# Attention softmax with eight score tiles instead of seven, one reciprocal tile instead of two, and no pad

## The chip, the cores and the metric

The kernel runs on one core of a Trainium2 chip. The metric is the time of one execution on the device in microseconds (us); less is better. The core has a matrix engine (TensorE, PE in the profile; PEld is its loading of weights, which overlaps with its matmuls), three engines for element-wise work (VectorE or DVE, ScalarE or ACT, GpSimd or POOL) and SyncE (SP), which here only issues transfers. POOL issues transfers too. Each engine takes its instructions in order. SBUF is the memory on the core that the engines work in, PSUM the one that matmuls write to.

## The reference

Two layers on a stream of 1024 latent positions and 256 context positions of width 1024, in float32. Layer 0 is attention, layer 1 a state-space mixer that the change does not touch. Around each stand a modulated RMS normalization and a gated residual add. The attention has 16 heads of 64 in four groups that share keys and values:

```python
s = jnp.einsum('bqkgd,bskd->bkgqs', qb, kb).astype(jnp.float32) * scale
p = sink_softmax(s, sink_kg, mask).astype(vb.dtype)
return jnp.einsum('bkgqs,bskd->bqkgd', p, vb)
...
y_lat = ((o * jax.nn.silu(g)) @ w_out).astype(h_lat.dtype)
```

A block of 128 latent queries looks at up to three blocks of 128 latent keys around it and at the two context blocks; context queries look at the context alone. `sink_softmax` adds one more logit per head to the sum of the exponentials.

## The kernel before

A product of two float32 matrices is made from three matmuls over a high and a low part of each operand: ACT rounds a weight tile to its high part (`split_w`, line 221) and DVE or POOL subtracts (line 223).

The attention works in 40 units, one for each block of 128 queries and each of the four key groups. The first 8 are context units with two key blocks each, the other 32 are latent units with four or five. A unit has two halves.

`att_front` (line 740) loads the unit's queries through POOL's queue (lines 748 and 753) and its gates through SP's (749). Then, for each of the four heads r of the group, PE computes the scores S in PSUM (lines 767 and 768; two S buffers), DVE scales, masks and reduces them to `sm` in SBUF (line 772) and ACT makes the exponential in place with its sum (774). A short chain follows: the sink's share (777, 778), the sum (779), its reciprocal (781) and a copy of the reciprocals spread out by POOL (`rs`, 782).

`att_back` (line 785) goes over the key blocks. PE transposes the four `sm` tiles' part of the block into `pt` (793; two buffers), ACT rounds it (`ph`, 797), DVE takes the low part (`pl`, 798), and PE multiplies both with the values into `pv` (799, 800). After the last block PE transposes `rs` (806), and DVE, ACT and POOL put the output of the unit together, with the reciprocals and the gates (807 to 816).

The main loop of `attention` (line 930) writes `att_front` of unit x+1 and then `att_back` of unit x. After each key block `tick` (903) advances a filler: the q and gate projections of the second half of the latent positions, and later the output projection of the blocks that are done (`proj_g`, lines 238 to 240; weights by `load_halves`, 245). The output projection of the last 512 positions comes behind the units; its weights are loaded into buffers of the tag `sm` (line 228, `spare`).

The order on each engine is not that of the program text. A planner at build time takes, for each engine, the instruction that was written first among those that it expects to be ready; the filler has a higher priority and may not be ahead of a given matmul (`issue_after`). It also places the waits. A tile's tag has a number of buffers (`BUFS`, line 41), which its tiles take in turn; a tile can be written once the tile that had its buffer before has been read for the last time. `sm` has 7 buffers of 2560 bytes per partition, `rs` has 2 of 1024 bytes. The pool `att` begins with a tile `pad` of 1536 bytes (line 826) that nothing writes or reads.

Of the kernel before, what the change touches and what calls it, by code (L numbers as in the profile page):

```python
# [9 lines left out]
F32 = mybir.dt.float32  # L10
# [7 lines left out]
P = 128  # L18
# [11 lines left out]
HD = 64  # L30
# [10 lines left out]
BUFS = dict(  # L41
    wr=2, wh=2, wl=2, arow=1, rr512=2, sqt=3, ut=3, ar=3, ah=2, al=2,
    pj=1, S=2, pt=2, pv=1,
    rope_b=2, qf=3, qh=3, ql=2, kHH=2, kLL=2, qs=2, sgt=2, sm=7, mx=2, nm=2, es=2, sums=2, ph=2, pl=2, co=1, ot=2,
    oraw=3, h1=2, h1k=8, wada=6, gq=1, sqa=1,
    cacc=2, cctx=1, bT=2, cT=2, xn4=4, xn2=1, bn4=4, bn2=1, sz=2, xw=2, hf=2, hx=2, M=2, bw=2, y2=1, xs=1, uT=2, pj2=2, psX=3, sk=2, dg=2,
)
# [66 lines left out]
class Kernel:  # L114
# [13 lines left out]
    def t(self, pool, shape, dt, tag, bufs=None):  # L128
        self.n += 1
        kw = {"bufs": bufs or BUFS.get(tag, 1)}  # L130
        return pool.tile(shape, dt, tag=tag, name=f"{tag}_{self.n}", **kw)
# [608 lines left out]
    def att_front(self, p, x, i, j, b):  # L740
        nc, t = self.nc, self.t
        ps = self.psA
        o = b * P - TT[i][0]
        sg = t(self.psm, [P, 2, P], F32, "sgt")
        nm = t(p, [P, R], F32, "nm")
        sums = t(p, [P, R], F32, "sums")
        qs = t(p, [P, R, P], F32R, "qs")
        nc.gpsimd.dma_start(qs, self.q_d[j][i][:, :, :, o : o + P].rearrange("e s d n -> (s d) e n"))
        nc.sync.dma_start(sg, self.sg_d[j][i][:, :, o : o + P].rearrange("e p n -> p e n"))

        z = j % 2
        qz = self.qz[z]
        nc.gpsimd.dma_start(qz[z * HD : (z + 1) * HD], self.q_d[j][i][:, z, :, o : o + P].rearrange("e d n -> d e n"))
        if b < 8:
            k0, k1 = max(b - 1, 0), min(b + 2, 8)
        else:
            k0, k1 = 8, 8
        kb = list(range(k0, k1)) + [8, 9]
        c0_ = 512 - (k1 - k0) * P
        m0 = {0: 128, 7: 640}.get(b, 0 if b < 8 else 384)  # L760
        W = len(kb) * P
        sms = []
        for r in range(R):
            S = t(self.psS, [P, 1024], F32, "S")
            for x, (qq, kk) in enumerate(((qs[:, r, :], self.kHH[j]), (qz[:, r, :], self.kL[j // 2]))):
                if k1 > k0:
                    nc.tensor.matmul(S[:, c0_:512], qq, kk[:, k0 * P : k1 * P], start=x == 0, stop=x == 1)  # L767
                scored = nc.tensor.matmul(S[:, 512:768], qq, kk[:, LAT : LAT + CTX], start=x == 0, stop=x == 1)  # L768
            self.scored.append(scored.ins)
            Sv = S[:, c0_:768]  # L770
            sm = t(self.psm, [P, 640], F32, "sm")
            nc.vector.tensor_tensor_reduce(out=sm[:, :W], in0=Sv, in1=self.mask[:, m0 : m0 + W], scale=-SCALE, scalar=self.nsink[:, 4 * j + r : 4 * j + r + 1],  # L772
                                           op0=ALU.add, op1=ALU.min, accum_out=nm[:, r : r + 1])
            nc.scalar.activation(sm[:, :W], sm[:, :W], AF.Exp, bias=nm[:, r : r + 1], scale=-1.0, accum_out=sums[:, r : r + 1])  # L774
            sms.append(sm)
        es = t(p, [P, R], F32, "es")
        nc.gpsimd.tensor_tensor(es, nm, self.sink[:, 4 * j : 4 * j + 4], op=ALU.add)
        nc.scalar.activation(es, es, AF.Exp)
        nc.gpsimd.tensor_tensor(sums, sums, es, op=ALU.add)
        rs = t(self.pb, [P, 2, 2, HD], F32, "rs", 2)  # L780
        nc.vector.reciprocal(sums, sums)
        nc.gpsimd.tensor_copy(rs, sums.rearrange("p (x e) -> p e x", e=2).unsqueeze(3).broadcast_to([P, 2, 2, HD]))
        return j, b, i, o, kb, sms, sg, rs
# [34 lines left out]
    def attention(self, c0, ckv):  # L818
        nc, t, a = self.nc, self.t, self.a
# [3 lines left out]
        self.psm = self.pool("sm", ctx=c0)  # L823
        self.pb = self.pool("back", ctx=c0)
        p = self.pool("att", ctx=c0)
        t(p, [P, 384], F32, "pad")
        cq = ExitStack()
        pq = self.pq = self.pool("qp1", ctx=cq)
        BUFS.update(qf=2, rope_b=1, qh=1, ql=1)
# [986 lines left out]
```

## Time and profile before

| | us |
|---|---|
| median of 3 runs | 1782.68 |
| lowest, highest | 1781.32, 1782.68 |
| the profiled execution, its time | 1780.27 |
| its span, first to last instruction | 1778.4 |

The mean granted clock of TensorE in the profiled execution is 0.996 of full speed. The attention's units begin at about 248 us and the transposes of the last end at about 676 us.

The profile names an instruction by its line (L793), engine, operation and tiles (written tile <- read tiles; 128x512 is partitions by elements). A row "A <- B: total, times, longest" says that instructions A waited for B, and how long. Rows in order of time have the start and the length in us, and in brackets the idle time of the engine ahead of the instruction, with what ended it. The ends of matmuls are modelled; a PE that is busy is not one at its peak.

### The profile page before, as it was taken

What the parts mean: (1) busy time and instruction counts of PE and PEld (TensorE: products, weight loads), DVE (VectorE), ACT (ScalarE), POOL (GpSimd) and SP (SyncE); (2) the same over time, 40 slices, a digit from 0 to 9 for tenths busy, and PEclk for the clock granted to TensorE, in tenths of its full rate; (3) what the DMA queues carried; (4) which work ended last, traced back from release to release, by engine and by line L of the source; (5) the groups of instructions that cost most, each with busy time, mean ns of one, the idle gap of its engine ahead of it and who ended that gap; (6) DMA issues with size and microseconds to landing.
All of it is one profiled execution on the core that took longest, in us unless ns stands there. A gap on an engine that the chain in (4) does not pass through costs nothing.

```text
span 1778.4 us, 29177 instructions
## 1 busy us (share of the span) xinstructions
PE 1739.9 (98%) x10413; PEld 1505.5 (85%) x10413; DVE 1204.2 (68%) x2119; ACT 871.8 (49%) x1902; POOL 796.8 (45%) x1066
## 2 busy tenths in 40 slices
PE   9999999999999999999999999999999999999997
PEld 6897788888888787778898898989889898988887
DVE  5744446788877875684876867677685767876634
ACT  4522247777777774352444444344443434544522
POOL 3231047555565545103454553636455363554321
PEclk9999999999999999999999999999999999999998
DMA  9478855444455446222323233332333333655533
GB/s 361 169 216 256 293 145 143 101 103 106 113 151 132 117 109 217 74 64 63 81 73 91 81 81 84 83 82 72 92 81 76 89 81 80 180 165 168 182 102 117
DMA packets 211388, 225.53 MB, mean 127 GB/s; under 512 B 15788, under 2 KB 149036, under 8 KB 211244
## 3 DMA queue, kind: packets, MB, share of 16 engines
q1 hardware_dynamic: 177180, 205.02, 39.0%
q0 software_dynamic: 34064, 18.65, 5.7%
q8 instruction: 82, 1.34, 0.3%
q14 instruction: 62, 0.51, 0.1%
HBM read 188.78 MB, written 35.13 MB: 126 GB/s over the span
## 4 chain that ended last, share of the span: by engine, by line
PE 84%; DVE 8%; DMA 2%; ACT 2%; issue 2%; POOL 1%; SPq 0%; DVEq 0%; ACTq 0%; POOLq 0%
PE pj L1213 18%; PE pj L1247 10%; PE pj L1648 7%; PE pj L238 6%; PE pj L239 6%; PE pj L240 6%; PE psD L1198 4%; PE psX L1400 3%; PE pt L793 3%; PE psD L1316 2%; PE pv L800 2%; PE psX L1369 2%; PE psX L1368 2%; PE pv L799 2%; PE S L767 1%
## 5 line engine op out<-in xcount | busy, mean ns | idle before, releaser
L238 PE MATMUL pj<-uH,wh 128*128 128x512 f32 (+1 forms) x680 | 244.1, 359 | 3.9 <-DVE h L859 2.0
L240 PE MATMUL pj<-uH,wl 128*128 128x512 f32 (+1 forms) x680 | 230.1, 339 | 1.4 <-POOL wl L223 1.4
L239 PE MATMUL pj<-uL,wh 128*128 128x512 f32 (+1 forms) x680 | 230.5, 339 | 0.4 <-POOL uL L816 0.4
L1213 PE MATMUL pj<-uH,wh 128*128 128x512 f32 x512 | 173.8, 411 | 1.2 <-ACT bn L1168 1.2
L1213 PE MATMUL pj<-uH,wl 128*128 128x512 f32 x512 | 170.4, 403 | 0.0
L1213 PE MATMUL pj<-uL,wh 128*128 128x512 f32 x512 | 168.2, 403 | 0.0
L1291 POOL TENSOR_TENSOR xw<-xn,dtdec 128x256 f32<-128x256 f32 x144 | 95.5, 664 | 160.4 <-PE psD L1316 75.8
L238 PEld LDWEIGHTS pj<-uH,wh 128*128 128x128 f32 x680 | 129.3, 190 | 28.0 <-ACT wh L221 5.7
L1247 PE MATMUL pj<-wh,uH 128*128 128x256 f32 x512 | 150.7, 294 | 0.0
L1247 PE MATMUL pj<-wl,uH 128*128 128x256 f32 x512 | 150.5, 294 | 0.0
L1247 PE MATMUL pj<-wh,uL 128*128 128x256 f32 x512 | 150.2, 293 | 0.0
L798 DVE TENSOR_TENSOR pl<-pt,ph 128x512 fp32r<-128x512 f32 x168 | 114.0, 688 | 47.2 <-ACT ph L797 46.2
L240 PEld LDWEIGHTS pj<-uH,wl 128*128 128x128 f32 x680 | 128.8, 190 | 17.3 <-POOL wl L223 2.2
L239 PEld LDWEIGHTS pj<-uL,wh 128*128 128x128 f32 x680 | 129.7, 191 | 10.5 <-issue 1.1
L223 POOL TENSOR_TENSOR wl<-wr,wh 128x512 fp32r<-128x512 f32 x74 | 97.2, 1316 | 84.7 <-ACT wh L221 83.8
L772 DVE CUSTOM_DVE_ANT_0 sm<-S,mask,nsink 128x640 f32<-128x640 f32 (+2 forms) x160 | 119.2, 772 | 20.6 <-PE S L768 13.5
L1432 ACT ACTIVATE uT<-psX,nw 128x128 f32<-128x128 f32 x128 | 46.5, 363 | 171.7 <-PE psX L1431 167.7
L774 ACT ACTIVATE sm<-sm,nm 128x640 f32<-128x640 f32 (+2 forms) x160 | 118.7, 742 | 17.5 <-DVE nm L772 16.9
L797 ACT CAST ph<-pt 128x512 fp32r<-128x512 f32 x168 | 97.4, 585 | 56.7 <-PE pt L793 52.4
L221 ACT CAST wh<-wr 128x512 fp32r<-128x512 f32 (+1 forms) x116 | 74.5, 648 | 81.8 <-PE pj L239 58.4
L1213 PEld LDWEIGHTS pj<-uH,wl 128*128 128x128 f32 x512 | 96.0, 188 | 19.9
L1213 PEld LDWEIGHTS pj<-uL,wh 128*128 128x128 f32 x512 | 95.5, 188 | 19.2
(352 smaller groups left out, 4945.3 us busy)
## 6 DMA issues: line engine op xcount, KB each, us to landing
wr<-w_x SPq DMA_DIRECT2D x32, 512.0 KB, 4.2
M<-acs SPq DMA_DIRECT2D x64, 256.0 KB, 5.3
bw<-acs SPq DMA_DIRECT2D x64, 256.0 KB, 5.6
wr<-w_sk SPq DMA_DIRECT2D x24, 512.0 KB, 4.1
wr<-wg SPq DMA_DIRECT2D x40, 256.0 KB, 5.2
qs<-q POOLq DMA_DIRECT2D x40, 256.0 KB, 3.9
wada<-w_ada SPq DMA_DIRECT2D x16, 512.0 KB, 8.6
wr<-wq SPq DMA_DIRECT2D x32, 256.0 KB, 3.1
```

The costliest lines, as they stand in the source:

```text
L223: (eng or nc.vector).tensor_tensor(l, raw, h, op=ALU.subtract)
L238: self.nc.tensor.matmul(ps, lh, rh, start=first and i == 0, stop=False)
L239: self.nc.tensor.matmul(ps, lh, rl, start=False, stop=False)
L240: self.last_mm = self.nc.tensor.matmul(ps, ll, rh, start=False, stop=last and i == n - 1)
L772: nc.vector.tensor_tensor_reduce(out=sm[:, :W], in0=Sv, in1=self.mask[:, m0 : m0 + W], scale=-SCALE, scalar=self.nsink[:, 4 * j + r : 4 * ...
L774: nc.scalar.activation(sm[:, :W], sm[:, :W], AF.Exp, bias=nm[:, r : r + 1], scale=-1.0, accum_out=sums[:, r : r + 1])
L797: nc.scalar.copy(ph, ptf)
L798: nc.vector.tensor_sub(pl, ptf, ph)
L1213: self.pe = nc.tensor.matmul(raw[:, 512 * i : 512 * i + 512], l[:, k, :], r[i][:, k, :], start=k + y == 0, stop=k == KT - 1 and y == 2)
L1247: self.pe = nc.tensor.matmul(pj[:, c], l, r[:, k, :], start=c % 2 + q + k + y == 0, stop=c % 2 == 1 and q == 1 and k == 3 and y == 2)
L1291: nc.gpsimd.tensor_tensor(xw, X(st, c).rearrange("p (r h) -> p r h", r=R), self.dtdec[:, c, hd(d, g)].unsqueeze(2).broadcast_to([P, R, HP] ...
L1648: self.pe = nc.tensor.matmul(banks[x], l[:, z, sl], r, start=k == 2 * qs[0] and y == 0, stop=k == 2 * qs[-1] + 1 and y == 2)
```

## The change

Three edits, all in the attention. The number of `sm` buffers goes from 7 to 8. The tile `rs` takes the default number of buffers of a tag without an entry, which is 1, in place of 2. The `pad` tile goes. Seven tiles of 2560 bytes, two of 1024 and the pad of 1536 are as many bytes as eight of 2560 and one of 1024. The planner plans the whole program again.

```diff
-    ... ql=2, kHH=2, kLL=2, qs=2, sgt=2, sm=7, mx=2, nm=2, es=2, sums=2, ph=2, pl=2, co=1, ot=2,
+    ... ql=2, kHH=2, kLL=2, qs=2, sgt=2, sm=8, mx=2, nm=2, es=2, sums=2, ph=2, pl=2, co=1, ot=2,
...
-        rs = t(self.pb, [P, 2, 2, HD], F32, "rs", 2)
+        rs = t(self.pb, [P, 2, 2, HD], F32, "rs")
         nc.vector.reciprocal(sums, sums)
         nc.gpsimd.tensor_copy(rs, sums.rearrange("p (x e) -> p e x", e=2).unsqueeze(3).broadcast_to([P, 2, 2, HD]))
...
         p = self.pool("att", ctx=c0)
-        t(p, [P, 384], F32, "pad")
         cq = ExitStack()
```

More of the change, by code (lines that the diff above doesn't have):

```diff
@@ L43 @@
     pj=1, S=2, pt=2, pv=1,
-    rope_b=2, qf=3, qh=3, ql=2, kHH=2, kLL=2, qs=2, sgt=2, sm=7, mx=2, nm=2, es=2, sums=2, ph=2, pl=2, co=1, ot=2,
+    rope_b=2, qf=3, qh=3, ql=2, kHH=2, kLL=2, qs=2, sgt=2, sm=8, mx=2, nm=2, es=2, sums=2, ph=2, pl=2, co=1, ot=2,
     oraw=3, h1=2, h1k=8, wada=6, gq=1, sqa=1,
```

## The prediction

> **What bounds the kernel now.** I read the page first, then the engines' busy time by stretch, then who waited for whom inside the attention, then one unit of it in order of time.
>
> ```profile
> PE 1739.9 (98%) x10413; PEld 1505.5 (85%) x10413; DVE 1204.2 (68%) x2119; ACT 871.8 (49%) x1902; POOL 796.8 (45%) x1066
> ...
> PE 84%; DVE 8%; DMA 2%; ACT 2%; issue 2%; POOL 1%; SPq 0%; DVEq 0%; ACTq 0%; POOLq 0%
> ```
>
> TensorE (PE) is busy in 98% of the span and holds 84% of the chain that ended last. The change touches the attention alone, so only its stretches matter. In the next view the columns are the length, then PE, weight loads, DVE, ACT and POOL busy, each with its instructions.
>
> ```profile
> 248.00:295.00 47.00, 45.59 (x249) 37.76 (x248) 30.80 (x100) 34.57 (x103) 32.29 (x52) 1.00 0.60 142
> 295.00:670.00 375.00, 364.05 (x2173) 310.89 (x2171) 292.34 (x622) 273.49 (x606) 214.07 (x306) 1.00 0.48 117
> 670.00:720.00 50.00, 46.93 (x206) 36.55 (x207) 31.06 (x40) 22.16 (x39) 25.75 (x21) 1.00 0.60 195
> ```
>
> The first row is the eight context units, the second the 32 latent units, the third the output projection behind them. PE idles 1.41, 10.95 and 3.07 us, together 15.4 us, 0.9% of the run. That is all that a better order can give back, unless it takes out work, and this change takes out none. DVE at 78% of the long stretch comes second.
>
> What PE waits for in the long stretch (total, times, longest; all six rows):
>
> ```profile
> PE pv L800 <- DVE pl L798: 5.4, 12, 1.9
> PE pj L238 <- DVE h L859: 2.0, 2, 1.6
> PE S L767 <- DVE nm L772: 0.7, 2, 0.5
> PE pv L799 <- DVE ot L812: 0.7, 1, 0.7
> PE pt L380 <- DVE dg L378: 0.4, 1, 0.4
> PE pv L799 <- ACT ph L797: 0.3, 1, 0.3
> ```
>
> No row has the transposes (L793) waiting for a softmax tile, which is what an eighth tile would serve.
>
> **The change part by part.** A unit u has four softmax tiles r0 to r3. Taking seven buffers in turn, the nth tile gets the buffer of tile n-7: r3 of unit u+1 that of r0 of unit u, and r0 of u+2 that of r1 of u. These come free when the last key block of u is transposed. The trace has it, in the order of time (start, length, and in brackets the idle time before):
>
> ```profile
> 427.26 0.60 PE L793 MATMUL pt<-ident,sm 128*128 128x128 f32 x4
> ...
> 427.57 0.88 DVE L772 CUSTOM_DVE_ANT_0 sm<-S,mask,nsink 128x640 f32<-128x640 f32 x1 [0.62 <-PE pt L793]
> ...
> 428.38 0.88 DVE L772 CUSTOM_DVE_ANT_0 sm<-S,mask,nsink 128x640 f32<-128x640 f32 x1
> ...
> 428.50 0.83 ACT L774 ACTIVATE sm<-sm,nm 128x640 f32<-128x640 f32 x1
> ...
> 428.85 0.38 PE L806 MATMUL pt<-ident,rs 128*128 128x128 f32 x2
> ...
> 429.19 0.68 DVE L798 TENSOR_TENSOR pl<-pt,ph 128x512 fp32r<-128x512 f32 x1
> ...
> 430.35 0.40 POOL L782 COPY rs<-sums 128x256 f32<-128x256 f32 x1 [0.56 <-DVE sums L781]
> ...
> 430.56 0.88 DVE L772 CUSTOM_DVE_ANT_0 sm<-S,mask,nsink 128x640 f32<-128x640 f32 x1 [0.27 <-PE S L768]
> ...
> 431.40 0.89 DVE L772 CUSTOM_DVE_ANT_0 sm<-S,mask,nsink 128x640 f32<-128x640 f32 x1
> ...
> 431.43 0.60 PE L793 MATMUL pt<-ident,sm 128*128 128x128 f32 x4
> ...
> 433.52 0.83 ACT L774 ACTIVATE sm<-sm,nm 128x640 f32<-128x640 f32 x1
> ...
> 434.67 0.50 PE L800 MATMUL pv<-pl,v 128*128 128x512 f32 x1
> ```
>
> The first transpose of the last block lets the reduction at 427.57 go: r3 of u+1; 428.38 is r0 of u+2; 430.56 and 431.40 are r1 and r2 of u+2, as soon as a score buffer S (there are two) is free again.
>
> *The eighth tile.* With eight, r0 of u+2 takes the buffer of r0 of u, and r3 of u+1 takes one that came free a whole unit earlier. So at 427.57 and 428.38 stand r0 and r1, at 430.56 and 431.40 r2 and r3. It is the same row of four reductions, set off by the same transpose and held by the same two score buffers, with the names moved on by one. Instructions added or removed: none on any engine; 160 reductions and 160 exponentials stay. What r3 gains is a lead of about one unit less 4 us. Who needed it? The next unit's first transpose, at 431.43. Its r3 exponential ended at 428.50 + 0.83 = 429.33, already 2.1 us earlier. That transpose has a second condition that stays: a transposed-block buffer, free again after pl of the last block at 429.19 + 0.68 = 429.87. So the earliest moment moves from 429.87 to 429.87. I take 0. Its lower end is that the replanned order removes all PE idle of the long stretch, -10.95 us; its upper end, where DVE's front work pushes pl back by one more reduction (0.88 us) in each of the 12 places in which PE already waits for pl, is +10.6 us. I take 0 because the nearest row, the transposes waiting for softmax, does not exist.
>
> *What follows r3.* Its small chain (sum, exponential of the sink, reciprocal, copy of the reciprocals, L777 to L782) goes from behind the first of the four reductions to behind the last, 431.40 - 427.57 = 3.8 us later within the row, for a unit whose end is then a unit farther away. It feeds only L806 at that unit's end. Cost 0, if nothing queues behind it; the next edit decides that.
>
> *One buffer for the reciprocals.* The copy (L782) for unit u+2 may now write only when unit u+1's transposes L806 have read the tile. Until now the copy came after that by itself: 428.85 + 0.38 is before 430.35. Now r3 of u+2 is reduced at 431.40 and its exponential ends at 433.52 + 0.83 = 434.35. Before the change 430.35 - 429.33 = 1.02 us lay between the end of r3's exponential and the copy; by that the copy could go at 435.4, an estimate. The L806 that it must let pass is that of the next unit:
>
> ```profile
> 440.82 0.38 PE L806 MATMUL pt<-ident,rs 128*128 128x128 f32 x2
> ```
>
> So the copy is held 441.2 - 435.4 = 5.8 us. It is not urgent, but it stands on POOL, in order: behind it wait weight splits (L223), the gating products (L813, L816) and the q loads that POOL issues (L748, L753). If the planner puts the copy behind L806, all of them pass and the cost is 0; if it is queued at its old place, it costs what POOL cannot absorb (rival B). I take 0: the planner orders an engine's queue by when it expects an instruction to be ready, and the wait is known to it.
>
> *The pad.* No instruction writes it. 2560 bytes for a tile = 1024 for the second reciprocal buffer + 1536 for the pad, so the tiles behind keep their places.
>
> *Context units.* Same rotation with two blocks per unit; PE idles 1.41 us there: 0, at best -1.4.
>
> *The output projection.* Its 16 weight halves go through the softmax buffers:
>
> ```profile
> 664.52 5.12 SPq L231 DMA_DIRECT2D sm<-wo  x4
> ...
> 673.67 6.75 SPq L231 DMA_DIRECT2D sm<-wo  x7
> ```
> ```profile
> PE pj L240 <- POOL wl L223: 1.4, 2, 1.1
> ...
> PE S L240 <- POOL wl L223: 0.2, 1, 0.2
> ```
>
> When the last unit holds four tiles, seven leave three for early loads and eight leave four, so the fourth half need not wait for a split to release a buffer. PE waits 1.4 + 0.2 us for splits there: between -1.6 and 0. I take 0, as those waits may be for later halves.
>
> Sum: 0 against the profiled 1780.27 us (span 1778.4). The median of the runs is 2.41 us above that, so I predict **1782.7 us**.
>
> [...]
>
> **The rivals.**
>
> *A, faster.* The first transpose of a unit no longer hangs on r3, and the planner puts it ahead of the scores between 429.77 and 431.43, so ph and pl of the first block come earlier and the wait before 434.67 goes. For it: the matmul at 434.67, which waits for pl, comes right behind such a burst of scores and reductions. Against: the 429.87 bound, and scores are traced earlier, so they go first. Price: the 5.4 us of the row: 1777.3. At most 10.95: 1771.7.
>
> *B, slower.* The held copy of the reciprocals. POOL is busy 214.07 of 375 us, so it has 160.9 / 32 = 5.0 us of slack a unit. A hold below that is absorbed; from 5.0 us on each further one goes into the splits and, through them, into PE, so a hold of 5.8 us costs 0.8 us. In a third of the latent units that is 8.5 us: 1791.2; in all 32, 25.6 us: 1808.3. For it: the hold is longer than the slack, and POOL is in order. Against: the planner knows the wait.
>
> *C, nothing moves.* The planner keeps its order and the buffer stays idle at the decisive moment: 1782.7.
>
> **How the numbers follow.** Forecast, the order moved by one reduction and its waits shuffled: 0.47, its own range 1778 to 1788; of it 0.35 fall within 0.2% (3.6 us, about what a measurement of this kernel can tell from no change), 0.05 below and 0.07 above. A 0.21, all of it faster. B 0.26, all of it slower. C 0.06, all within. Together: faster 0.26, same 0.41, slower 0.33. The range leaves out A's far end and B beyond some 13 of the 32 units (13.5 x 0.8 = 10.8 us above 1782.7): 1774 to 1793.5.
>
> **What would show it.** Right: PE idle of the latent units near 11 us; the reduction behind the last block's transposes is followed at once by a second, and both belong to one unit; the copies L782 stand behind L806. Rival A: the row of pv waiting for pl well under 5.4 us, and the first transposes of a unit ahead of its scores. Rival B: a row of the copy waiting for pt L806, and PE waiting for POOL's splits inside the attention, where no such row stands now. I am wrong if PE idle changes by over 4 us with neither.

## The result and the profile after

The changed kernel takes 1774.41 us (median of 4 executions, 1771.74 to 1776.79) against 1782.63 us before; the ratio is 0.9955 with the interval 0.9938 to 0.9972. In a later set, with 9 executions beside 33 of the kernel before, it is 0.9978 (0.9963 to 0.9993), 1776.58 against 1780.78 us. So the change is faster, by 4 to 8 us, and 0.2 to 0.5% is near the limit of what can be told here. The forecast was no change.

The busy times of the same three stretches, after (columns as before):

```profile
248.00:295.00 47.00, 44.87 (x248) 37.20 (x247) 30.77 (x102) 34.97 (x104) 32.53 (x54) 1.00 0.60 138
295.00:670.00 375.00, 365.59 (x2179) 312.97 (x2178) 289.13 (x623) 273.21 (x607) 213.11 (x305) 1.00 0.48 119
670.00:720.00 50.00, 47.84 (x213) 37.57 (x212) 31.35 (x41) 21.63 (x37) 25.80 (x21) 1.00 0.58 189
```

PE idles 2.13, 9.41 and 2.16 us, together 13.7 us for 15.4. That is 1.7 us, a third of what the two profiles differ by (spans of 1778.4 and 1773.2 us). So part of the gain lies outside these stretches. What PE waits for in the long one, after:

```profile
PE pv L800 <- DVE pl L798: 4.0, 12, 0.7
PE pj L238 <- DVE h L858: 2.5, 2, 2.1
PE pv L799 <- DVE ot L812: 1.2, 2, 0.6
```

The total of the first row fell from 5.4 to 4.0 us at the same 12 times, and its longest from 1.9 to 0.7 us: one wait went, not a little of each. That is the first thing to follow up.

To find the rest, the run is best cut at events and not at times. The first scores, the last transposes and the first matmul psD of layer 1, before:

```profile
248.00 0.40 PE L768 MATMUL S<-kHH,qs 128*128 128x256 f32 x2
...
675.10 0.60 PE L793 MATMUL pt<-ident,sm 128*128 128x128 f32 x4
...
738.77 0.38 PE L1198 MATMUL psD<-uH,wh 128*128 128x256 f32 x1 [1.13 <-ACT cacc L1032]
```

and after (a line behind the pad's now has a number less by one):

```profile
247.88 0.28 PE L768 MATMUL S<-kHH,qs 128*128 128x256 f32 x1
...
673.77 0.60 PE L793 MATMUL pt<-ident,sm 128*128 128x128 f32 x4
...
733.80 0.38 PE L1197 MATMUL psD<-uH,wh 128*128 128x256 f32 x1 [1.13 <-ACT cacc L1031]
```

The attention's units take 427.10 us before and 425.89 after, what lies between them and psD 63.67 and 60.03, and what follows psD to the end of the span 1039.6 and 1039.4. So in these two profiles the smaller part of the gain is in the units and the larger one behind them. A second profile of the changed kernel (`after_again` in the table below) has it the other way: 3.8 us in the units and 1.9 behind them. Both places count. The prediction's stretches, which end at 720 us, don't reach the second. Among the waits of PE there, before and after:

```profile
PE pj L238 <- ACT cacc L1032: 2.2, 1, 2.2
```
```profile
PE pj L238 <- ACT cacc L1031: 1.0, 1, 1.0
```

This is PE at the second projection of w_dt. Its PSUM buffer is emptied by four bias additions on ACT (cacc, line 1032), and those stand on ACT behind the rounding of the first w_x, the first weights of layer 1. The order of time before (SP issues the load, ACT rounds it, PE goes on):

```profile
721.96 0.43 SPq L1138 DMA_DIRECT2D wr<-w_x  x1
...
726.23 0.95 PE L360 MATMUL pt<-ones,sqa 128*128 128x1 f32 x8
726.90 1.04 ACT L1142 CAST wh<-wr 128x1024 fp32r<-128x1024 f32 x1 [1.79 <-DMA wr<-w_x]
727.85 1.47 ACT L1032 ACTIVATE cacc<-pj,db 32x128 f32<-32x128 f32 x4
...
729.37 0.50 PE L238 MATMUL pj<-uH,wdth 128*128 128x512 f32 x1 [2.19 <-ACT cacc L1032]
...
730.30 0.63 PE L238 MATMUL pj<-uH,wdth 128*128 128x512 f32 x1
730.73 0.63 PE L239 MATMUL pj<-uL,wdth 128*128 128x512 f32 x1
```

Behind the wait matmuls start 0.43 us apart, for 0.23 elsewhere. The column PEclk says why (725 to 730, then 730 to 735, before):

```profile
725.00:730.00 5.00, 2.81 (x23) 2.64 (x23) 1.92 (x2) 3.15 (x8) 0.31 (x1) 1.00 0.55 198
730.00:735.00 5.00, 5.00 (x17) 3.90 (x16) 1.83 (x2) 0.54 (x1) 0.70 (x1) 0.66 0.74 206
```

The granted clock falls to 0.66 for 5 us, some 1.7 us lost. After the change it stays at 1.00 there. It fell elsewhere, behind a wait of 2.1 us for h (L858, above):

```profile
495.00:503.00 8.00, 5.86 (x35) 5.52 (x34) 3.78 (x9) 4.05 (x9) 2.80 (x3) 0.79 0.57 143
```

Such drops come and go between executions, and the times scatter with them: of the 35 executions of the kernel before beside the first four experiments, 7 with a mean clock of 0.997 took 1778.6 us on average, 14 with 0.996 took 1780.2, and 12 with 0.995 took 1782.2.

### The profile page after: what moved, and what is told of

The parts are those of the page before. It is cut to its first block, busy times and chain, and to the rows that moved or that the text cites. A ratio compares the mean times of both kernels' runs of the same rounds, so it can differ in the third digit from the quotient of the medians.

```text
span 1773.2 us, 29238 instructions
## 1 busy us (share of the span) xinstructions
PE 1736.4 (98%) x10413; PEld 1503.1 (85%) x10413; DVE 1198.7 (68%) x2119; ACT 871.4 (49%) x1902; POOL 794.9 (45%) x1066
## 4 chain that ended last, share of the span: by engine, by line
PE 85%; DVE 7%; DMA 3%; ACT 2%; issue 2%; POOL 0%; SPq 0%; DVEq 0%; ACTq 0%; POOLq 0%
PE pj L1212 19%; PE pj L1246 10%; PE pj L1647 7%; PE pj L238 7%; PE pj L239 6%; PE pj L240 6%; PE psD L1197 4%; PE psX L1399 3%; PE pt L793 3%; PE psD L1315 2%; PE pv L800 2%; PE pv L799 2%; PE S L767 2%; PE psX L1368 2%; PE psX L1367 2%
## 5 line engine op out<-in xcount | busy, mean ns | idle before, releaser
L223 POOL TENSOR_TENSOR wl<-wr,wh 128x512 fp32r<-128x512 f32 x74 | 96.9, 1312 | 80.6 <-ACT wh L221 73.0
```

The lines of the kernel that those rows point to most:

```text
L223: (eng or nc.vector).tensor_tensor(l, raw, h, op=ALU.subtract)
```

## The experiments

Each label is a kernel; edits are against the kernel before unless said otherwise, and a counter that only keeps the tiles' names the same is left out of them. Ratios are to executions of the kernel before on the same chip, with 9 to 12 executions of the kernel (the first row `after` has 4 beside 4). An order that is called the same is that of the instructions on each engine. The segments of every trace, cut as above, come first, since the verdicts are read from them. "L301" is the length of the DVE step L301 near 618 us, "wait" that of PE for cacc, "drops" the first of the 5 us slices in which the granted clock was low (first score to psD), "sum" the three segments less the mean of the kernel before's two (1530.3 us), "runs" the median less that of the kernel before.

| kernel | units | to psD | rest | L301 | wait | drops | sum | runs |
|---|---|---|---|---|---|---|---|---|
| before | 427.10 | 63.67 | 1039.63 | 3.25 | 2.2 | 730 | | |
| again | 426.91 | 63.63 | 1039.67 | 3.50 | 2.3 | 730 | | -0.2 |
| after | 425.89 | 60.03 | 1039.40 | 0.48 | 1.0 | 495 | -5.0 | -8.2 |
| after_again | 423.26 | 61.78 | 1039.67 | 0.48 | 1.3 | 725 | -5.6 | -4.2 |
| units_only | 424.27 | 67.16 | 1039.88 | 0.48 | 3.5 | 690, 725 | +1.0 | -1.0 |
| tail_last | 424.33 | 65.67 | 1040.23 | 0.50 | 3.0 | 725 | -0.1 | -1.6 |
| rs1_only | 424.80 | 62.57 | 1039.14 | 0.65 | 0.8 | 690 | -3.8 | -3.5 |
| rs1_same | 424.29 | 63.07 | 1040.63 | 0.82 | 2.0 | 725 | -2.3 | -2.2 |
| rs3 | 422.90 | 64.26 | 1039.12 | 0.63 | 3.4 | 725 | -4.0 | -3.3 |
| nop1 | 423.49 | 64.67 | 1039.66 | 0.74 | 3.1 | 730 | -2.5 | -0.2 |
| nop2 | 426.04 | 65.70 | 1040.03 | 0.94 | 3.6 | 250, 725 | +1.5 | +0.1 |
| nop40 | 424.62 | 65.72 | 1039.75 | 0.59 | 3.0 | 725 | -0.2 | +0.1 |
| chain33 | 426.28 | 61.66 | 1039.68 | 2.68 | 1.7 | none | -2.7 | -1.3 |
| warm_before | 426.96 | 64.79 | 1039.14 | 3.29 | 1.5 | 730 | +0.6 | +0.4 |
| dve_before | 426.75 | 60.48 | 1039.71 | 3.41 | 0.8 | none | -3.4 | -2.9 |
| rs1_dve | 428.06 | 61.26 | 1040.76 | 0.48 | 0.8 | 620 | -0.2 | -3.1 |
| nop1_dve | 423.66 | 60.52 | 1039.73 | 0.66 | 0.8 | none | -6.4 | -3.1 |
| units_dve | 424.67 | 61.30 | 1039.42 | 0.48 | 0.8 | none | -4.9 | -5.9 |
| dve_after | 425.89 | 59.60 | 1039.92 | 0.48 | 0.8 | 500 | -4.9 | -6.2 |
| gpdve_after | 423.68 | 62.58 | 1040.20 | 0.47 | 0.4 | 725 | -3.8 | -2.2 |

**The parts alone.** `units_only` has the changed attention, with an eighth softmax tile that the output projection may not use; on PE, DVE, ACT, POOL and SP its units stand as in the changed kernel.

```diff
-            sm = t(self.psm, [P, 640], F32, "sm")
+            self.nsm = getattr(self, "nsm", 0) + 1; sm = t(self.psm, [P, 640], F32, "sx" if self.nsm % 8 == 4 else "sm")
-        rs = t(self.pb, [P, 2, 2, HD], F32, "rs", 2)
+        rs = t(self.pb, [P, 2, 2, HD], F32, "rs")
-        t(p, [P, 384], F32, "pad")
```

> Attention of the changed kernel, output projection of the old: every eighth softmax tile has a slot of its own that the spare weight halves may not use, one buffer for rs, no pad. Theory T (the gain lies mostly behind attention: the last transposes come 1.3 us earlier by the reordered units, the rest comes from the eighth slot's early weight load, a shorter wait for the first w_x cast and the clock behind it): 1.0 to 2.5 us below the kernel before, last transposes L793 near 674, the wait of PE for cacc still near 2 us. Rival U (the reordered units give it all): 5 to 8 us below. Rival N (nothing but scatter of the phases): within 1 us, either sign.

0.9996 (0.9987 to 1.0005). The units are 2.7 us shorter, and behind them 3.5 us are given back: PE waits longer for cacc, and the clock falls twice.

`tail_last` gives the eighth slot to the output projection alone.

```diff
-        t(p, [P, 384], F32, "pad")
+        self.sx = lambda: t(p, [P, 640], F32, "sx"); self.sx()
-            sm = t(self.psm, [P, 640], F32, "sm")
+            self.nsm = getattr(self, "nsm", 0) + 1; sm = self.sx() if self.nsm == 156 else t(self.psm, [P, 640], F32, "sm")
-            raw = self.t(self.psm, [P, 640], F32, "sm")[:, : kt * cols].rearrange("p (k c) -> p k c", k=kt)
+            self.nsp = getattr(self, "nsp", 0) + 1; raw = (self.sx() if self.nsp % 8 == 4 else self.t(self.psm, [P, 640], F32, "sm"))[:, : kt * cols].rearrange("p (k c) -> p k c", k=kt)
-        rs = t(self.pb, [P, 2, 2, HD], F32, "rs", 2)
+        rs = t(self.pb, [P, 2, 2, HD], F32, "rs")
```

> The old order of all units but the last two, the pad's place made a tile that the last softmax tile of the last unit but one uses and that then takes every eighth spare weight half, one buffer for rs. So a fourth weight half of the output projection loads early, as after the change. Theory T: the projection ends 0.9 us earlier, the wait for cacc falls from 2.2 us to near 1 and the slow matmuls behind 730 go: 2.5 to 4 us below the kernel before. Rival U (units): 0 to 0.5 us below. Rival C (the clock drop has nothing to do with the wait): about 1 to 2 us below, with the drop still in the trace.

0.9996 (0.9984 to 1.0008). The theory's wait of 1 us did not come (3.0 us). The units are shorter by 2.7 us, where their order, but for the last two and one row on POOL, is the old one. That points at the one buffer for rs, which stands alone in `rs1_only`.

```diff
-        rs = t(self.pb, [P, 2, 2, HD], F32, "rs", 2)
+        rs = t(self.pb, [P, 2, 2, HD], F32, "rs")
-        t(p, [P, 384], F32, "pad")
+        t(p, [P, 640], F32, "pad")
```

> Seven softmax tiles, one buffer for rs, a pad of 640 floats so that everything else lies where it lay; PE, DVE, ACT and SP are given the same order as before, and on POOL one copy L782 moves behind a weight split. Theory T and the prediction's step on rs: no change, within 0.7 us. Rival B of the prediction (a held copy delays POOL's splits): 2 to 9 us slower, with waits of PE for POOL's splits.

0.9979 (0.9970 to 0.9987), faster, with the same order on PE, DVE, ACT and SP and one row moved on POOL. My theory and the prediction's step both said no change. Since PE's order is the same, its matmuls can be compared one by one. Between the 619th and the 620th us of the kernel before the lead of `rs1_only` grows from 0.9 to 2.8 us; over the 10 us ahead of that it changes by 0.2. Before, DVE's, POOL's and PE's rows near 618 us:

```profile
617.71 0.63 POOL L753 DMA_DIRECT2D qz<-q  x1
618.04 3.25 DVE L301 SCALAR_TENSOR_TENSOR uL<-h,mod,uH 128x256 fp32r<-128x256 f32 x1
...
618.34 0.75 POOL L813 TENSOR_TENSOR ot<-ot,sgt 128x256 f32<-128x256 f32 x1
619.03 1.29 POOL L223 TENSOR_TENSOR wl<-wr,wh 128x512 fp32r<-128x512 f32 x1
620.28 0.71 POOL L816 TENSOR_TENSOR uL<-ot,uH 128x256 fp32r<-128x256 f32 x1
621.21 1.27 DVE L798 TENSOR_TENSOR pl<-pt,ph 128x512 fp32r<-128x512 f32 x2
...
621.94 0.50 PE L800 MATMUL pv<-pl,v 128*128 128x512 f32 x1 [1.90 <-DVE pl L798]
```

L301, the low half of a modulated tile, takes 3.25 us for 0.48. It ends 0.3 us behind the last of three POOL steps that stand back to back, pl is late, and here is the 1.9 us of the row of waits. With one buffer L301 takes 0.65 us. `rs1_same` and `nop1` below gain the same 1.8 to 1.9 us at the same matmul.

**What holds L301.** `rs1_same` keeps every tile's address, with an unused tile in the place of the second rs.

```diff
-        rs = t(self.pb, [P, 2, 2, HD], F32, "rs", 2)
+        rs = t(self.pb, [P, 2, 2, HD], F32, "rs"); t(self.pb, [P, 2, 2, HD], F32, "rt")
```

> One buffer for rs with an unused tile in the place of the second, so every other tile has the address it had; the orders are those of the run with one buffer and a larger pad: one POOL row moved. Rival A (the addresses decide whether POOL holds DVE near 618): the step L301 takes over 3 us there again and the time is within 1 us of the kernel before. Theory O (the one buffer itself, by order or waits): L301 at 0.5 to 0.7 us and 2 to 4 us below, like the earlier run. Rival P (chance of the phase in each execution): a mixture, the median between.

0.9990 (0.9978 to 1.0002). In its trace the step is short, so the addresses alone don't decide it:

```profile
616.89 0.82 DVE L301 SCALAR_TENSOR_TENSOR uL<-h,mod,uH 128x256 fp32r<-128x256 f32 x1
616.91 0.63 POOL L753 DMA_DIRECT2D qz<-q  x1
...
617.55 0.75 POOL L813 TENSOR_TENSOR ot<-ot,sgt 128x256 f32<-128x256 f32 x1
```

`chain33` shortens POOL's run by one step.

```diff
-        nc.gpsimd.tensor_tensor(oL[i][:, 2 * j : 2 * j + 2, o : o + P], ot, oh, op=ALU.subtract)
+        (nc.vector if (b, j) == (6, 1) else nc.gpsimd).tensor_tensor(oL[i][:, 2 * j : 2 * j + 2, o : o + P], ot, oh, op=ALU.subtract)
```

> The kernel before with one instruction moved: the subtraction L816 of the unit of block 6 and pair 1 on DVE for POOL, the last of three POOL steps that stand back to back near 618 to 621. Theory P (POOL's run of steps holds the DVE step L301, which starts only when POOL falls idle): L301 near 618 ends about 0.3 us behind the end of the weight split L223, at 2.4 to 2.7 us for 3.3, PE's longest wait for pl falls from 1.9 to about 1.2, 0 to 1 us below the kernel before. Rival F (L301's length has nothing to do with POOL): 3.2 to 3.5 us again. Rival Q (chance of the phase): 0.5 to 0.8.

```profile
616.49 2.68 DVE L301 SCALAR_TENSOR_TENSOR uL<-h,mod,uH 128x256 fp32r<-128x256 f32 x1
...
617.59 1.29 POOL L223 TENSOR_TENSOR wl<-wr,wh 128x512 fp32r<-128x512 f32 x1
...
619.83 0.50 PE L800 MATMUL pv<-pl,v 128*128 128x512 f32 x1 [1.32 <-DVE pl L798]
```

As theory P said: L301 ends at 619.17, 0.3 us behind L223's end at 618.88, and PE's wait is 1.3 us. 0.9991 (0.9980 to 1.0002). In the kernel before it ends at 621.29, as far behind L816's end at 620.99. So in these two traces POOL's run of steps holds L301 until POOL falls idle; in the kernel before one instruction waited through three others (0.75, 1.29 and 0.71 us). What it is in them that holds it, no run shows.

Four kernels move POOL's instructions: `rs3` has three buffers for rs and no pad (so no copy waits for PE; its order differs on every engine up to 320 us and is the old one behind that). The other three keep every other order: `nop40` has a memset of one column of the pad written behind each copy L782 (the planner put all 40 at 248 to 270 us), `nop1` a single one ahead of the attention, at 245 us, and `nop2` two. The edits of `rs3`, `nop40` and `nop1`:

```diff
-        rs = t(self.pb, [P, 2, 2, HD], F32, "rs", 2)
+        rs = t(self.pb, [P, 2, 2, HD], F32, "rs", 3)
-        t(p, [P, 384], F32, "pad")
```
```diff
-        nc.gpsimd.tensor_copy(rs, sums.rearrange("p (x e) -> p e x", e=2).unsqueeze(3).broadcast_to([P, 2, 2, HD]))
+        nc.gpsimd.tensor_copy(rs, sums.rearrange("p (x e) -> p e x", e=2).unsqueeze(3).broadcast_to([P, 2, 2, HD])); nc.gpsimd.memset(self.scr[:, x : x + 1], 0.0)
-        t(p, [P, 384], F32, "pad")
+        self.scr = t(p, [P, 384], F32, "pad")
```
```diff
-        t(p, [P, 384], F32, "pad")
+        self.scr = t(p, [P, 384], F32, "pad"); nc.gpsimd.memset(self.scr[:, 0:1], 0.0)
```

> Seven softmax tiles, three buffers for rs, no pad: no copy L782 waits for a transpose, as with two. Theory R (what frees L301 is the wait for PE that each copy gets with one buffer): L301 near 618 at 3.2 to 3.5 us again, PE's longest wait for pl about 1.9, time within 1 us of the kernel before. Rival N (any other number of buffers than two moves POOL's program a little and frees it too): L301 at 0.5 to 0.8, 2 to 3 us below.

> The kernel before with one more POOL instruction behind each copy L782, a memset of one column of the pad, 128x1. Theory R: L301 near 618 at 3.2 to 3.5 us again. Rival N (the place of POOL's instructions in its program decides): 0.5 to 0.8 us, and the attention 2 us shorter.

> The kernel before with a single POOL memset of 128x1 ahead of the attention's first units and nothing else. Theory R: L301 near 618 at 3.2 to 3.5 us again, time within 0.7 us of the kernel before. Rival N (the place of POOL's instructions in its program decides, and one more shifts all that follow): 0.5 to 0.8 us and 2 us below.

> The kernel before with two POOL memsets of 128x1 ahead of the attention. Theory N (only the place of POOL's instructions in its program decides whether L301 gets in ahead of L813): L301 at 0.5 to 0.8 us as with one, or, where a small period decides, 3.2 to 3.5 again; either way the attention is 427 us from first score to last transpose with the long one and 423 to 425 with the short one. Rival V (the one short L301 with a single memset was chance of that execution): nothing to tell it from the kernel before.

The step is short in all four (0.59 to 0.94 us), rival N. With `nop1`:

```profile
617.84 0.63 POOL L753 DMA_DIRECT2D qz<-q  x1
617.90 0.74 DVE L301 SCALAR_TENSOR_TENSOR uL<-h,mod,uH 128x256 fp32r<-128x256 f32 x1
...
618.48 0.75 POOL L813 TENSOR_TENSOR ot<-ot,sgt 128x256 f32<-128x256 f32 x1
```

It gets in between POOL's issue of qz and L813: in all eight traces with POOL's instructions in this order and a short step (these four, `tail_last`, `rs1_only`, `rs1_same` and `nop1_dve`) it ends 0.17 to 0.18 us behind the end of that issue. In all five traces with POOL's instructions where they were, it did not; L301 stood 0.08 to 0.33 us behind the start of qz there and -0.14 to 0.31 where it got in (`tail_last`, `rs1_only`, `rs1_same`, the four here), so these starts don't decide it. Between `nop1` and the kernel before one POOL instruction some 370 us earlier is the only difference, and it does. Through what, stays open. The ratios are 0.9982 (0.9972 to 0.9993) for `rs3`, but 1.0000, 0.9998 and 0.9998 for the memsets (intervals of about 0.0012 to each side), so the 2 us that rival N had for them did not come, and rival V is right in time alone: their wait for cacc is 3.0 to 3.6 us, and `to psD` grows by 1 to 2 us. For `nop1` the sum of its own trace, -2.5 us, is still more than its runs show.

**The wait for w_x.** `dve_before` takes the four bias additions from ACT, where they stood behind the rounding of w_x, to DVE.

```diff
-            self.nc.scalar.activation(dst[sl], pj[sl, q % 2 * n : q % 2 * n + n], AF.Identity, bias=self.dtbias[sl])
+            src = pj[sl, q % 2 * n : q % 2 * n + n]; self.nc.vector.tensor_scalar(out=dst[sl], in0=src, scalar1=self.dtbias[sl], scalar2=None, op0=ALU.add) if n == 128 else self.nc.scalar.activation(dst[sl], src, AF.Identity, bias=self.dtbias[sl])
```

> The kernel before with the four bias additions of the context positions (L1032, PSUM to cacc) on DVE for ACT, where they stood behind the cast of the first w_x; nothing else moves but one DVE row. PE's 2.2 us wait for cacc should be gone. If the slow clock behind 730 is the answer to that wait (theory T): the wait (2.2) and the slow matmuls (1.5 to 2) both go, 3 to 4 us below the kernel before, granted clock 0.95 or more from 730 to 735. If the clock has its own phase (rival C): at most 2.2 us below, and the drop of the clock shows again somewhere near. If the time is taken up by the next wait (rival W: the weights' cast is late for the front's first matmuls anyway): under 1 us.

```profile
PE pj L238 <- DVE cacc L1032: 0.8, 1, 0.8
```
```profile
725.00:730.00 5.00, 4.17 (x28) 3.70 (x28) 3.19 (x6) 2.26 (x3) 1.88 (x1) 1.00 0.58 200
730.00:735.00 5.00, 4.45 (x18) 2.93 (x16) 1.83 (x2) 1.34 (x3) 0.00 (x1) 1.00 0.73 209
```

0.9983 (0.9974 to 0.9993): `to psD` is 3.2 us shorter, of it 1.4 by the wait and the other 1.8 by the clock, which did not fall. `warm_before` was to separate the two.

```diff
+                if i == 2:
+                    with self.tc.issue_after(self.last_mm.ins):
+                        wt = t(ps, [P, 512], F32, "pv")
+                        for _ in range(8):
+                            nc.tensor.matmul(wt, self.wdt[0][:, 0, :], self.uH[0][:, 0, :], start=True, stop=True)
```

> The kernel before with eight idle matmuls (128x512, 0.23 us each, their result unused) put between the 256-wide and the 512-wide projections of w_dt, in the place where PE waits about 2.2 us for cacc. The wait's end isn't moved. Theory H (the granted clock falls because PE is thinly used there): PE is kept busy through the wait, no drop of the clock from 725 to 740, the matmuls behind run at 0.23 us, 1 to 2.5 us below the kernel before, the full wait still there as busy time. Rival C (the drop has its own phase): the drop shows again within 15 us, time within 0.7 us of the kernel before.

1.0000 (0.9989 to 1.0011), and the clock fell. But w_x landed later in this execution and a wait of 1.5 us stayed behind the idle matmuls, so it doesn't tell the theories apart. The table speaks for theory H: of the traces with a wait of 1.3 us or more 11 of 12 have a drop from 725 to 740 us (`chain33` has none), of the eight with 1.0 or less only `gpdve_after`, which has another wait of 1.6 us there. By the slices' clocks a drop lost 1.7 us in seven of the eleven and 3.4 us in the other four, whose waits were 3.0 to 3.6 us (`units_only`, `tail_last`, `nop2`, `nop40`). Why a drop comes in one trace and not in another, no run shows: PE waited 1.3 us for cacc in `after_again`, with a drop, and 1.7 us in `chain33`, without one.

**Both kernels as they are, and combinations.** `after_again` and `again` are the two kernels without an edit.

> The changed kernel as it is, for more runs and a second profile. Theory T2 (formed on the runs so far: the change takes away three things of the attention's end, a DVE step L301 that POOL held for 3.3 us near 618, part of PE's wait for cacc near 727, and the slow matmuls that followed that wait): 4 to 7 us below the kernel before, L301 near 618 at 0.5 to 0.7 us, the wait near 1 us. Rival S (the four runs shown with the result were lucky, times scatter with the clock): 0 to 3 us below.

> The kernel before as it is, for a second profile. Theory T2: the step L301 near 618 takes about 3.3 us again, PE waits about 2 us for cacc near 727 and the granted clock falls behind it. Rival S: at least one of the two is gone in this profile, so that it is chance and not the kernel's order.

Both came as theory T2 said, but that in `after_again` the clock fell at 725 us. `dve_after` and `units_dve` are the changed kernel and `units_only` with the DVE step, `gpdve_after` adds to the first the four loads ahead of w_x on POOL's queue, `rs1_dve` and `nop1_dve` are `rs1_only` and `nop1` with the DVE step (no eighth tile). The edit of `gpdve_after`, the same for cb, nw and dsk:

```diff
-        nc.sync.dma_start(self.cw, a["conv_w"].rearrange("p (t j) -> p t j", t=32))
+        nc.gpsimd.dma_start(self.cw, a["conv_w"].rearrange("p (t j) -> p t j", t=32))
```

> The changed kernel with the four bias additions of the context positions (L1032) on DVE for ACT, so that they no longer stand behind the cast of the first w_x. If that wait still costs the changed kernel its 1 us and now and then a drop of the clock (theory T2): 0.5 to 2.5 us below the changed kernel, 5 to 9 below the kernel before. If the landing of w_x is early enough after the change (rival W): within 0.5 us of the changed kernel.

> Attention of the changed kernel, output projection with three early weight halves as before the change, the bias additions on DVE. Beside the changed kernel with the same DVE step only one weight load on SP and three small steps stand elsewhere. Theory E (the fourth early half is worth about 0.5 us of PE's waits in the output projection): 0.2 to 1 us above that kernel, 4 to 6 below the kernel before. Rival Z (the slot is worth nothing there): level with it. Rival M (the slot carries most of what is left): 2 us or more above.

> The changed kernel with the bias additions on DVE and the four loads of constants (L979, L982, L985, L987), which stand ahead of the first w_x on SP, issued by POOL. If the landing of w_x still sets something (rival W): 0.5 to 2 us below the changed kernel with the DVE step alone. Theory T2 (that wait is then the drain of the bias additions alone): within 0.7 us of it; 5 to 8 us below the kernel before either way.

> Seven softmax tiles, one buffer for rs (pad 640), and the four bias additions on DVE: no eighth tile anywhere. Theory T2 (what the change brought is the step L301 freed near 618 and the shorter wait for the first w_x, with the clock behind it): 4 to 6 us below the kernel before, within 1 us of the changed kernel with the same DVE step. Rival E (the eighth tile brings time of its own through the reordered units or the fourth early weight half): 2 to 3 us below only, 2 us or more above the changed kernel with the DVE step.

> The kernel before with one POOL memset of 128x1 ahead of the attention and the bias additions on DVE: nothing of the change is in it, neither the eighth tile nor the one buffer. If L301 freed near 618 (2 to 3 us) and the wait for the first w_x with its clock (2 to 3 us) are what the change brought (theory T3): 4 to 6 us below the kernel before, within 1 us of the changed kernel. Rival E2 (the eighth tile is worth 2 us or more): 2 to 4 us below only. Rival G (what the attention gains is given back behind it): 2 to 3 us below.

0.9970 (0.9959 to 0.9981), 0.9968 (0.9954 to 0.9982), 0.9981 (0.9970 to 0.9993), 0.9980 (0.9967 to 0.9992) and 0.9985 (0.9974 to 0.9997). `dve_after` is 2 us below the changed kernel on the same chip (1774.58 and 1776.58 us), and `units_dve` is 5.9 us below the kernel before: the two lowest of the five. Without the wait for w_x the fourth early half is worth nothing (rival Z), while between `units_only` and the changed kernel, with that wait, it is 3 us (-1.0 and -4.2, on two chips). `gpdve_after` gained 2.2 us, less than the 5 to 8 that both its theories had: POOL's queue for the constants brought a wait for the sum of squares (1.6 us) in place of what it saved. `rs1_dve` and `nop1_dve` stay some 3 us above `dve_after` and `units_dve`, as rivals E and E2 say (rival G's 2 to 3 us is close too, but the trace of `nop1_dve` gives nothing back behind the units); `nop1_dve` and `units_dve` ran on one chip, and their intervals overlap a little. But in the traces the eighth tile makes the units no shorter: 423.7 us in `nop1_dve` and 424.7 in `units_dve`. (The units of `rs1_dve`, 428.1 us, are long although L301 is short: DVE waits 2.1 us for a load of h at 615 us, and the clock falls at 620.) Where these 3 us lie isn't seen in the traces kept, so a worth of the eighth tile is not ruled out.

## Why the prediction was wrong, step by step

- **What bounds the kernel.** That PE bounds it held. The bound of 15.4 us on what can be given back was drawn too narrowly. It ended at 720 us, before the first weights of layer 1, which stand in SP's and ACT's queues behind the change's own loads; there the two profiles differ by 3.6 us. And it counted idle time alone, while a drop of the clock costs 1.7 us or more in which PE is busy.
- **The eighth tile in the units, 0.** Right, as far as the traces show. The pattern came as worked out, with two reductions behind the last transposes and two behind the score buffers, after:

```profile
425.95 0.88 DVE L772 CUSTOM_DVE_ANT_0 sm<-S,mask,nsink 128x640 f32<-128x640 f32 x1 [0.62 <-PE pt L793]
...
426.76 0.88 DVE L772 CUSTOM_DVE_ANT_0 sm<-S,mask,nsink 128x640 f32<-128x640 f32 x1
...
428.94 0.89 DVE L772 CUSTOM_DVE_ANT_0 sm<-S,mask,nsink 128x640 f32<-128x640 f32 x1 [0.36 <-PE S L768]
...
429.78 0.88 DVE L772 CUSTOM_DVE_ANT_0 sm<-S,mask,nsink 128x640 f32<-128x640 f32 x1
```

  The rows have no buffer numbers; that the first two belong to one unit follows from the count of buffers alone. With L301 free and no drop of the clock the units take 422.9 to 424.8 us with seven tiles (`rs1_only`, `rs1_same`, `tail_last`, `rs3`, `nop1`, `nop40`, `nop1_dve`) and 423.3 to 424.7 with eight (`after_again`, `units_only`, `units_dve`, `gpdve_after`). No run has the eighth tile beside two buffers for rs.
- **The held copy, 0.** This is the first step that failed. The copies stand behind L806, as forecast, and PE has no wait for POOL's splits in the units:

```profile
POOL rs L782 <- PE pt L806: 32.2, 19, 3.2
```

  Rival B is out. But the 0 was given no lower end, as if moving a row on POOL could only cost time, and this edit alone frees L301: 2.7 us in the units at the same addresses (`rs1_same`). It is no property of one buffer, since three buffers or one memset do it too. In the changed kernel the whole order is new, and L301 stands 2.2 us behind the start of qz there. An earlier L301 takes longer there, 2.17 us for 1.21 near 603, at no wait of PE over 0.7 us for pl.
- **Rival A** named the right row and the wrong cause: the row of pl fell well below 5.4 us (4.0; 3.5 in `after_again`), by its one wait of 1.9 us, which POOL made, and not by transposes moved ahead of scores. I had quoted the longest wait and not looked at it. That rival A's price, 1777.3 us, lies near the measured times is luck.
- **The output projection, -1.6 to 0, taken as 0.** This is the second step that failed: the term was closed at the waits for splits. Those waits themselves fell by 0.3 us only (one of 1.1 us stays in the row for pj), but the earlier fourth half also shortens what stands behind it: w_x was issued 2.2 us ahead of the first w_dt matmul (719.02 and 721.24) for 1.5 before (721.96 and 723.43), was rounded 4.5 us after its issue for 4.9, and PE's wait fell from 2.2 to 1.0 us; in one of the two profiles the drop of the clock went with it. Between `units_only` and the changed kernel this slot is the only difference, and `to psD` is 5 to 7 us shorter. But `units_only` has a wait that neither the kernel before nor the changed one has: SP's first load of constants (L979), which stands ahead of w_x, waits 2.4 us there until POOL's last split has ended. `tail_last`, with a fourth early half and the old units, shows no gain (w_x issued 1.3 us ahead of the first w_dt matmul and rounded after 5.6 us). In the traces with the additions on ACT, w_x is rounded 4.5 to 6.3 us after its issue (6.2 in `units_only`), and what sets that is not known, so the link from the slot to w_x is not settled.
- **Pad and context units, 0.** No run left out the pad alone; planned without it, the order of every engine's instructions is the same. PE idles 0.7 us more in the context units.
- **"Wrong if PE idle changes by over 4 us with neither."** In the latent units it changed by 1.5 us, so by its own sign the prediction looked right inside the attention while the time moved behind it.

## What to carry to other kernels

Look at the longest wait of a row before pricing the row: one of 1.9 us among twelve has a cause of its own, here a DVE step of 3.25 us, where 0.48 is the shortest of its shape. Cut the run at events, and follow a change through each in-order queue up to the first load of the next stage: time won in the attention was given back there in the kernels where that load was late. And where a few microseconds move after an edit that should cost nothing, try an edit that does nothing, such as one memset, before crediting the edit.

## What the runs showed of the hardware

- The DVE step L301 near 618 us (128x256), 0.48 us at its shortest, took 3.25 to 3.5 us beside three POOL steps that followed each other without a gap (`before`, `again`, `warm_before`, `dve_before`), and ended 0.3 us behind them (621.29 and 620.99 in `before`); beside two such steps (`chain33`) it took 2.68 and ended 0.3 us behind the second. With a single POOL memset of 128x1 ahead of the attention it took 0.74 and 0.66 us (`nop1`, `nop1_dve`).
- Beside a POOL instruction that issues a DMA the same step ended 0.17 to 0.18 us behind the end of that instruction, in eight traces of eight with a short step there.
- Between 725 and 740 us the granted clock fell in 11 of the 12 traces in which PE waited 1.3 to 3.6 us for cacc, and in one of the eight with 1.0 us or less (`gpdve_after`, where PE waits 1.6 us for the sum of squares). By the slices' clocks seven of the eleven drops lost 1.7 us and four 3.4. Ahead of the wait stand 0.95 us of 128x1 matmuls (L360, `before`).
- One thousandth of the mean granted clock goes with some 1.7 us of the time (35 executions of one kernel).
